# A block's second SiLU, gating and split behind the next block's first product, in a fused encoder layer on one core

## The chip, the core and the metric

The kernel is one launch on one core of a Trainium2 chip. A core has TensorE (PE in the rows, with its weight loads apart as PEld), VectorE (DVE), ScalarE (ACT), GpSimd (POOL) and SyncE (SP, which here issues the DMAs). Each engine works through its own instructions in the order in which the program wrote them, and waits on semaphores for the others. The metric is the device time of the launch in microseconds: 1426.03 us, the median of three runs (1423.1 to 1428.0).

## The reference, cut to what matters

One encoder layer over 1024 positions of 1024 features, fp32: two kinds of attention, then a gated MLP with a depthwise convolution over three positions. The change is in the MLP:

```python
h = modulate(rms_norm(x), shift_ffn, scale_ffn)
gate, val = jnp.split(causal_depthwise_conv(h @ w_up, conv_w, conv_b), 2, axis=-1)
x = x + gate_ffn[:, None, :] * ((jax.nn.silu(gate) * val) @ w_down)
...
return rms_norm(x) * final_g
```

`w_up` is 1024 x 5632 and `w_down` 2816 x 1024, so there are 22 blocks of 128 gate columns, each with its 128 value columns.

## The kernel before

The MLP fills the second half of the launch. Positions lie along the free axis in two halves of 512 (`lo`, `hi`). Every fp32 operand of a matmul is split into a rounded high part and the remainder (`wh` and `wl`, `ah` and `al`, `dh` and `dl`), and a product is made of three matmuls per 128 rows of depth: high by high, high by low, low by high. A split takes a rounding copy and a subtraction.

The blocks from the third on (`act_fast`, `fb` = 2 to 21, 20 of them) use seven products of 12 matmuls instead of eight, by sums and differences of weights and of activations that are made beforehand. They go into four PSUM tiles, X, Y, W and Z (all named `up` in the trace):

- first product, X = w0 by B11; ACT copies X to SBUF (L1154, `y<-up`);
- second, Y; DVE adds it to that copy (L1164), which is the first half of the gate columns; ACT starts its convolution (L1133), DVE ends it (two rows of L1137), ACT takes the SiLU (L1172);
- a second product *into X* (w4 by T2, `up<-Tc,wh` in the rows), which adds onto what stands there: it can't begin before ACT has read X (L1154). ACT copies X again (L1170);
- the "third product" of the change, again into X (w5 by B12, line 1181, `up<-h,wh`): it needs L1170 done. ACT copies X a third time (L1182);
- W, Z and Z again: DVE takes them off (L1188, L1198, L1209), ACT and DVE do the convolutions of the value columns and of the second half of the gate columns, ACT takes the second half's SiLU (L1214).

`gated` (line 1067) multiplies one half of gate and value (L1070, DVE), rounds the product to `ah` (L1071, a cast on DVE before) and subtracts for `al` (L1072, DVE). It is called for the first half at line 1207 and for the second at line 1218.

The way down of block b (`down`, 16 tiles of three matmuls, `dnf<-...` in the rows, and a DVE addition L1262 into `x2`) is spread between the products of block b + 1 by `tiles(n)`; `NDOWN` says how many tiles go into each place, four more stand at the block's end. Tiles 0 to 3 and 8 to 11 use the first half's `ah`, `al`, the others the second half's; tiles 0 to 7 use the first half of the `w_down` columns (`dh`, `dl`), 8 to 15 the second. These are made from a loaded piece `modt` by POOL (L1237, times the gate), ACT (L1239, `dh`) and POOL (L1240, `dl`). Three `modt` buffers exist and two hold constants, so the load of the second half starts when L1240 of the first is done. The splits of the next block's `w_up` (ACT L1092, POOL L1094) and the sums of its weights (POOL L1101 to L1106) run in between; the split behind the first product makes w5 and w6.

All of these calls are kept in the order written (`ko`, `keep_in_program_order`), engine by engine, so the order of the Python statements is the order on each engine.

Of the kernel before, what the change touches and what calls it, by code (L numbers as in the profile page):

```python
# [13 lines left out]
AF = mybir.ActivationFunctionType  # L14
# [12 lines left out]
NP = 8  # L27
FF = 2816
NF = FF // P
NDOWN = 2, 3, 2, 2, 3  # L30
NLAST = 2, 2, 0, 0, 0
NTWO = 0, 4, 2, 3, 3
TL = sum(NLAST)
# [22 lines left out]
def build(nc, tc, t, ctx):  # L56
    sy, ve, sc, gp, te = nc.sync, nc.vector, nc.scalar, nc.gpsimd, nc.tensor
    cnt = [0]

    def mk(pool, shape, dt, tag):  # L60
        cnt[0] += 1
        return pool.tile(shape, dt, name=f"{tag}_{cnt[0]}", tag=tag, bufs=BUFS.get(tag, 1))
# [61 lines left out]
    def load_w(src, shape):  # L124
        raw = mk(wst, shape, F32, "raw")
        r = sy.dma_start(raw, src)
        if hold[0]:
            tc.keep_in_program_order(r)
        return raw
# [98 lines left out]
    ko = tc.keep_in_program_order  # L228
# [834 lines left out]
    def act_tiles(last):  # L1063
        return [[mk(p2, [P, HALF], F32R, "h2") if last else mk(p3, [P, HALF], F32R, n) for _ in range(2)]
                for n in ("ah", "al")]

    def gated(yg, yv, hf, ah, al):

        cc = slice(hf * HALF, (hf + 1) * HALF)
        ko(ve.tensor_mul(yg[:, cc], yg[:, cc], yv[:, cc]))  # L1070
        ko(ve.tensor_copy(ah[hf], yg[:, cc]))  # L1071
        ko(ve.tensor_sub(al[hf], yg[:, cc], f(ah[hf])))  # L1072


# [10 lines left out]
    def weight_sums(fb, w):  # L1085

        rv, rg = (load_w(t["w_up"][b], [P, KB, P]) for b in (NF + fb, fb))
        g0, g1, v0, v1 = rg[:, 0:4], rg[:, 4:8], rv[:, 0:4], rv[:, 4:8]

        def split(tag, pl, raw, cuts=None):  # L1090
            wh, wl = (mk(pl, list(raw.shape), F32R, tag + x) for x in "hl")
            ko(sc.copy(wh, raw))  # L1092
            for a, z in cuts or [(0, raw.shape[1])]:
                late.append(lambda a=a, z=z: ko(gp.tensor_sub(wl[:, a:z], raw[:, a:z], f(wh[:, a:z]))))  # L1094
            late.pop(-len(cuts) if cuts else -1)()
            w.extend([x[:, n:n + 4] for x in (wh, wl)] for n in range(0, raw.shape[1], 4))

        yield
        split("w", p0, rg)
        yield  # L1100
        ko(gp.tensor_sub(g0, g0, v0))  # L1101
        ko(gp.tensor_add(v0, v0, v1))
        yield
        split("wq", p3, v1)
        ko(gp.tensor_sub(v1, v1, g0))
        ko(gp.tensor_sub(g1, v1, g1))  # L1106
        yield
        split("w", p0, rv, fb == 2 and ((4, 8), (0, 4)))
        yield
        split("w", p0, rg, fb == 2 and ((0, 4), (4, 8)))  # L1110

    late = []

    def roundrobin(*its):
        while True:
# [4 lines left out]
    def run(it, n):  # L1120
        for _ in range(n):
            next(it, None)

    def product(ps, w, b, start):
        n = 0
        for kb in LO:
            for x, y in ((0, 0), (0, 1), (1, 0)):
                ko(te.matmul(ps, w[x][:, kb], b[kb][y], start=start and n == 0, stop=n == 11, skip_group_check=True))  # L1128
                n += 1

    def conv_steps(y, src, b, a, z):
        b = slice(b, b + 1)
        ko(sc.activation(y[:, a:z], src[:, a:z], AF.Identity, scale=cw[2][:, b], bias=cb[:, b]))  # L1133
        for d in (1, 2):
            yield
            o = max(a, d)
            ko(ve.scalar_tensor_tensor(y[:, o:z], src[:, o - d:z - d], cw[2 - d][:, b], y[:, o:z], ALU.mult, ALU.add))  # L1137

    def act_fast(fb, w, dn, nw, nw1, ld, ld1, act, after, last):


        X, Y, W, Z = (mk(fps[0][1], [P, HALF], F32, "up") for _ in range(4))
        lo, hi = slice(0, HALF), slice(HALF, S)
        n = NLAST if last else NTWO if fb == 2 else NDOWN
        cg, cv = (mk(p2, [P, S], F32, "y") for _ in range(2))
        nx = lambda it: next(it, None)

        def tiles(n, c=iter(()), dn=dn):
            for _ in range(n):
                nx(dn)  # L1150
                nx(c)

        product(X, w[0], B11, True)
        ko(sc.copy(cg[:, lo], X))  # L1154
        if fb == 2:
            second_act()
        yg, yv = (mk(p2, [P, S], F32, "y") for _ in range(2))
        nx(nw)
        nx(nw1)
        product(Y, w[1], B21, True)  # L1160
        while late:
            late.pop(0)()
        nx(ld)
        ko(ve.tensor_add(cg[:, lo], Y, cg[:, lo]))  # L1164
        c = conv_steps(yg, cg, fb, 0, HALF)
        if fb > 2:
            nx(c)
        tiles(n[0], c)
        product(X, w[4], T2, False)
        ko(sc.copy(cg[:, hi], X))  # L1170
        run(c, 9)
        ko(sc.activation(yg[:, lo], yg[:, lo], AF.Silu))  # L1172
        nx(nw1)
        nx(ld)
        if fb == 2:
            nx(ld)
        if last:
            nx(ld1)
            fg.append(load_w(bass.AP(t["final_g"].tensor, 0, [[0, P], [1, D]]), [P, D]))
        tiles(n[1])  # L1180
        product(X, w[5], B12, False)
        ko(sc.copy(cv[:, hi], X))  # L1182
        nx(nw1)
        if last:
            nx(ld1)
        tiles(n[2])
        product(W, w[2], T4, True)
        ko(ve.tensor_sub(cv[:, lo], cv[:, hi], W))  # L1188
        c = conv_steps(yv, cv, NF + fb, 0, HALF)
        nx(c)  # L1190
        if last:
            nx(ld1)
        nx(nw1)
        tiles(n[3], c)
        run(c, 1 if last else 9)
        nx(ld1)
        product(Z, w[3], T1, True)
        ko(ve.tensor_sub(cv[:, hi], cv[:, hi], Z))  # L1198
        run(c, 9)
        c = conv_steps(yv, cv, NF + fb, HALF, S)  # L1200
        nx(c)
        nx(ld1)
        nx(nw1)
        tiles(n[4], c)
        run(c, 9)
        act += act_tiles(last)
        gated(yg, yv, 0, *act)
        product(Z, w[6], B22, False)
        ko(ve.tensor_sub(cg[:, hi], cg[:, hi], Z))  # L1209
        c = conv_steps(yg, cg, fb, HALF, S)  # L1210
        nx(c)
        nx(ld1)
        tiles(2 if last else 4, c, after)
        ko(sc.activation(yg[:, hi], yg[:, hi], AF.Silu))  # L1214
        nx(ld1)
        if last:
            tiles(3, dn=after)
        gated(yg, yv, 1, *act)

    gbc = []  # L1220

# [43 lines left out]
    def down(a, w, order):  # L1265
        for tb, hf in order:
            down_mm(tb, hf, [a], [w])
            yield
# [37 lines left out]
    def conv_half(y, src, b, hf):  # L1306
        b = slice(b, b + 1)
        a, z = hf * HALF, (hf + 1) * HALF
        ko(sc.activation(y[:, a:z], src, AF.Identity, scale=cw[2][:, b], bias=cb[:, b]))
        for d in (1, 2):  # L1310
            yield
            ko(ve.scalar_tensor_tensor(y[:, a + d:z], src[:, 0:HALF - d], cw[2 - d][:, b], y[:, a + d:z], ALU.mult,
                                       ALU.add))

    def conv_join(y, before, b):

        b = slice(b, b + 1)
        for d in (1, 2):
            o = y[:, HALF:HALF + d]
            ko(ve.scalar_tensor_tensor(o, before[:, HALF - d:HALF], cw[2 - d][:, b], o, ALU.mult, ALU.add))  # L1320
# [14 lines left out]
    lo, hi = slice(0, HALF), slice(HALF, S)  # L1335
# [42 lines left out]
    yg, yv = (mk(p2, [P, S], F32, "y") for _ in range(2))  # L1378
    act = act_tiles(False)
# [6 lines left out]
    for kb in LO:  # L1386
        split2(T1[kb], sums[kb])
    gated(yg, yv, 0, *act)
    run(ld, 1)

# [46 lines left out]
    yg, yv = (mk(p2, [P, S], F32, "y") for _ in range(2))  # L1437
# [6 lines left out]
    dn = down(act, wd, by_half)  # L1444
# [16 lines left out]
    def second_act(yg=yg, yv=yv, act=act1):  # L1461
        conv_join(yg, g0, 1)
        ko(sc.activation(yg, yg, AF.Silu))
        run(conv_half(yv, v0, NF + 1, 0), 9)
        conv_join(yv, v0, NF + 1)
        for hf in range(2):
            gated(yg, yv, hf, *act)

    act, wd = act1, wd1
    for fb in range(2, NF):  # L1470
        last = fb == NF - 1
        w1 = []
        nw1 = iter(()) if last else weight_sums(fb + 1, w1)
        wd1 = [], []
        ld1 = load_down(fb, wd1, last)
        dn, act1 = down(act, wd, by_half), []
        if last:
            dn = islice(dn, TL)
            out = chain(dn, down_last((act, act1), (wd, wd1)))
        act_fast(fb, w, dn, nw, nw1, ld, ld1, act1, out if last else dn, last)  # L1480
        act, w, nw, wd, ld = act1, w1, nw1, wd1, ld1
# [39 lines left out]
```

## Time and profile before

| what | number |
|---|---|
| median of three runs | 1426.03 us |
| the profiled execution, its own time | 1425.51 us |
| its span, first to last instruction | 1423.5 us |
| PE busy over the span | 1309.2 us (92%), 6644 matmuls |
| DVE busy | 1176.2 us (83%) |
| ACT busy | 617.2 us (43%) |
| POOL busy | 864.9 us (61%) |

The table is the page's head and first part. A share of busy time is a mean over stages with different limits, and a matmul's end is modelled, so a PE that is shown busy may still lose time: the starts of two matmuls, one behind the other, tell what was lost between them. Rows of the timeline give the start in us from the span's start, how long it took, engine, line, operation, what it writes and reads, and at the end, in brackets, the idle time before it and who ended it; x2 at the end of a row merges two instructions.

### The profile page before, as it was taken

How to read it: one execution, taken by the hardware profiler on the slowest of the kernel's cores; microseconds unless marked ns; L12 is line 12 of the kernel's file. 1: busy time of each engine (PE TensorE's matmuls, PEld its weight loads, DVE VectorE, ACT ScalarE, POOL GpSimd, SP SyncE). 2: the span in 40 equal slices, each digit the busy share in tenths (PEclk: the TensorE clock that was granted, in tenths of full speed). 3: DMA queues.
4: the chain of work that ended last, by engine and by line, in shares of the span. 5: the costliest groups of instructions: out<-in, count | busy, mean ns of one | idle time of the engine just before them, and what ended most of it. 6: DMA issues, size and time to landing. Idle time of an engine off the chain costs nothing.

```text
span 1423.5 us, 19845 instructions
## 1 busy us (share of the span) xinstructions
PE 1309.2 (92%) x6644; PEld 1083.0 (76%) x6644; DVE 1176.2 (83%) x1967; ACT 617.2 (43%) x1270; POOL 864.9 (61%) x760
## 2 busy tenths in 40 slices
PE   4889999999899978798887999999999999999996
PEld 2688998898778966676665877777777778777774
DVE  7858777677778868876889889999998889899887
ACT  5647567575545433333432333323333333333334
POOL 4646576765333436563578667776676677667664
PEclk9999999999999999899998999999999999999998
DMA  8534433414665686665011111111111111211213
GB/s 311 180 100 112 104 88 85 119 49 120 166 167 144 179 263 197 217 193 193 22 45 36 47 52 45 45 45 60 52 54 58 45 45 45 60 52 49 62 37 119
DMA packets 80047, 144.57 MB, mean 102 GB/s; under 512 B 10041, under 2 KB 36809, under 8 KB 79946
## 3 DMA queue, kind: packets, MB, share of 16 engines
q1 hardware_dynamic: 79946, 143.31, 33.9%
q8 instruction: 53, 0.87, 0.3%
q14 instruction: 48, 0.39, 0.1%
HBM read 102.89 MB, written 18.88 MB: 86 GB/s over the span
## 4 chain that ended last, share of the span: by engine, by line
PE 43%; DVE 35%; ACT 7%; issue 5%; DMA 5%; POOL 4%; SPq 1%; POOLq 0%; DVEq 0%; ACTq 0%
PE mm L136 14%; PE up L1128 12%; DVE y L1137 8%; PE T L136 6%; PE dnf L136 6%; DVE x L1262 4%; PE S L136 3%; ACT y L1133 3%; DVE ah L1071 3%; DVE y L1070 2%; DVE adaw L254 1%; DVE macc L918 1%; PE up L1302 1%; POOL wl L121 1%; DVE al L1072 1%
## 5 line engine op out<-in xcount | busy, mean ns | idle before, releaser
L1262 DVE TENSOR_TENSOR x<-dnf,x 128x512 f32<-128x512 f32 x340 | 222.5, 679 | 1.6 <-PE dnf L136 1.6
L1137 DVE SCALAR_TENSOR_TENSOR y<-y,sm,y 128x512 f32<-128x512 f32 (+2 forms) x160 | 187.3, 1171 | 28.8 <-ACT y L1133 28.7
L1128 PE MATMUL up<-h,wh 128*128 128x512 f32 x640 | 199.7, 393 | 2.6 <-ACT y L1170 1.8
L1094 POOL TENSOR_TENSOR wl<-raw,wh 128x1024 fp32r<-128x1024 f32 (+1 forms) x62 | 160.1, 2583 | 66.1 <-ACT wh L1092 59.5
L1133 ACT ACTIVATE y<-y,sm 128x512 f32<-128x512 f32 x80 | 65.3, 817 | 254.7 <-DVE y L1209 133.4
L136 PE MATMUL mm<-H,wh 128*128 128x512 f32 x448 | 150.2, 403 | 0.0
L1128 PEld LDWEIGHTS up<-h,wh 128*128 128x128 f32 x640 | 119.7, 189 | 31.1 <-ACT y L1170 5.2
L136 PE MATMUL dnf<-dh,ah 128*128 128x512 f32 x336 | 133.5, 397 | 10.0 <-DVE x L1262 8.8
L136 PE MATMUL dnf<-dl,ah 128*128 128x512 f32 x336 | 134.0, 399 | 3.7 <-POOL dl L1240 2.5
L802 POOL TENSOR_TENSOR pb<-pb,kt 128x512 f32<-128x512 f32 (+2 forms) x96 | 89.4, 945 | 77.0 <-DVE kt L799 50.0
L136 PE MATMUL dnf<-dh,al 128*128 128x512 f32 x336 | 132.6, 395 | 0.9 <-DVE al L1072 0.9
L1128 PE MATMUL up<-h,wl 128*128 128x512 f32 x320 | 125.3, 392 | 0.0
L822 DVE TENSOR_TENSOR ptl<-T,pth 128x512 fp32r<-128x512 f32 (+2 forms) x192 | 98.5, 517 | 30.7 <-ACT pth L821 29.0
L821 ACT CAST pth<-T 128x512 fp32r<-128x512 f32 (+2 forms) x192 | 87.4, 457 | 62.3 <-PE T L136 60.9
L795 POOL TENSOR_SCALAR pb<-pb,ri 128x640 f32<-128x640 f32 (+2 forms) x64 | 45.4, 711 | 106.2 <-DVE ri L794 67.7
L136 PE MATMUL mm<-wh,H 128*128 128x256 f32 x512 | 102.8, 292 | 6.6 <-DVE vs L511 6.6
L799 DVE TENSOR_TENSOR_SCAN kt<-kt 128x128 f32<-128x128 f32 (+3 forms) x64 | 98.2, 1534 | 9.8 <-ACT kt L784 9.4
L1128 PE MATMUL up<-Tc,wh 128*128 128x512 f32 x320 | 100.9, 396 | 4.6 <-ACT y L1154 4.5
L1240 POOL TENSOR_TENSOR dl<-modt,dh 128x512 fp32r<-128x512 f32 x42 | 65.3, 1554 | 64.3 <-ACT dh L1239 64.3
L1237 POOL TENSOR_TENSOR modt<-modt,modt 128x512 f32<-128x512 f32 x44 | 68.8, 1563 | 58.2 <-DMA modt<-w_down 58.2
L136 PE MATMUL S<-kh,qs 128*128 128x384 f32 (+5 forms) x352 | 99.5, 364 | 4.6 <-ACT pb L778 4.4
L136 PE MATMUL T<-ident,pb 128*128 128x128 f32 x528 | 91.1, 277 | 8.8 <-POOL pb L802 3.5
(214 smaller groups left out, 3451.1 us busy)
## 6 DMA issues: line engine op xcount, KB each, us to landing
raw<-w_up SPq DMA_DIRECT2D x44, 512.0 KB, 3.6
rawm<-ada SPq DMA_DIRECT2D x128, 128.0 KB, 2.4
qs<-ex SPq DMA_DIRECT2D x104, 128.0 KB, 2.5
modt<-w_down SPq DMA_DIRECT2D x44, 256.0 KB, 2.7
adaw<-ada SPq DMA_DIRECT2D x16, 512.0 KB, 5.7
raw<-w_qk SPq DMA_DIRECT2D x16, 512.0 KB, 3.6
kh<-ex SPq DMA_DIRECT2D x56, 128.0 KB, 2.6
tbd<-wh SPq DMA_DIRECT2D x18, 256.0 KB, 2.6
```

What stands on the lines that cost most here:

```text
L136: r = fn(*a, **k)
L799: ve.tensor_tensor_scan(r, r, r, 1.0, ALU.mult, ALU.bypass)
L802: gp.tensor_mul(pt[:, a:b], pt[:, a:b], kt[:, a + 1:b + 1])
L821: sc.copy(dh, tp[:, 0:b - a])
L822: ve.tensor_sub(dl, tp[:, 0:b - a], f(dh))
L1094: late.append(lambda a=a, z=z: ko(gp.tensor_sub(wl[:, a:z], raw[:, a:z], f(wh[:, a:z]))))
L1128: ko(te.matmul(ps, w[x][:, kb], b[kb][y], start=start and n == 0, stop=n == 11, skip_group_check=True))
L1133: ko(sc.activation(y[:, a:z], src[:, a:z], AF.Identity, scale=cw[2][:, b], bias=cb[:, b]))
L1137: ko(ve.scalar_tensor_tensor(y[:, o:z], src[:, o - d:z - d], cw[2 - d][:, b], y[:, o:z], ALU.mult, ALU.add))
L1237: ko(gp.tensor_mul(raw, raw, gbc[hf]))
L1240: ko(gp.tensor_sub(wl, raw, f(wh)))
L1262: r = ve.tensor_add(xc, ps, xc)
```

## The change

Three edits. The second half's SiLU, gating and split of a block are wrapped in `second_half` and put on a list; the next block calls them right behind its first product's copy, before its second product is written. (`second_act`, which did the same by a special case for the second block, comes through the same list.) The last block calls them where they were. One tile of the way down is moved from the place ahead of the third product to the place behind it (`NDOWN`). And the rounding copy to `ah` in `gated` goes from DVE to ACT, in all 44 uses.

```diff
--- before.py
+++ after.py
@@ -27,7 +27,7 @@
 NP = 8
 FF = 2816
 NF = FF // P
-NDOWN = 2, 3, 2, 2, 3
+NDOWN = 2, 2, 3, 2, 3
 NLAST = 2, 2, 0, 0, 0
 NTWO = 0, 4, 2, 3, 3
 TL = sum(NLAST)
@@ -1068,7 +1068,7 @@
 
         cc = slice(hf * HALF, (hf + 1) * HALF)
         ko(ve.tensor_mul(yg[:, cc], yg[:, cc], yv[:, cc]))
-        ko(ve.tensor_copy(ah[hf], yg[:, cc]))
+        ko(sc.copy(ah[hf], yg[:, cc]))
         ko(ve.tensor_sub(al[hf], yg[:, cc], f(ah[hf])))
 
 
@@ -1109,7 +1109,7 @@
         yield
         split("w", p0, rg, fb == 2 and ((0, 4), (4, 8)))
 
-    late = []
+    late, rest = [], []
 
     def roundrobin(*its):
         while True:
@@ -1152,8 +1152,7 @@
 
         product(X, w[0], B11, True)
         ko(sc.copy(cg[:, lo], X))
-        if fb == 2:
-            second_act()
+        rest.pop()()
         yg, yv = (mk(p2, [P, S], F32, "y") for _ in range(2))
         nx(nw)
         nx(nw1)
@@ -1211,11 +1210,17 @@
         nx(c)
         nx(ld1)
         tiles(2 if last else 4, c, after)
-        ko(sc.activation(yg[:, hi], yg[:, hi], AF.Silu))
-        nx(ld1)
+
+        def second_half(between=lambda: None):
+            ko(sc.activation(yg[:, hi], yg[:, hi], AF.Silu))
+            between()
+            gated(yg, yv, 1, *act)
+
         if last:
-            tiles(3, dn=after)
-        gated(yg, yv, 1, *act)
+            second_half(lambda: (nx(ld1), tiles(3, dn=after)))
+        else:
+            nx(ld1)
+            rest.append(second_half)
 
     gbc = []
 
@@ -1467,6 +1472,7 @@
             gated(yg, yv, hf, *act)
 
     act, wd = act1, wd1
+    rest.append(second_act)
     for fb in range(2, NF):
         last = fb == NF - 1
         w1 = []
```

The order on ACT at a block's boundary, before: L1214 is the second half's SiLU, L1154 the copy of the next block's first product, L1092 a weight split, L1239 a `dh`, L1133 and L1170 the convolution's start and the second copy of X.

```order
L1133 ACTIVATE y_10917<-y_10902,sm_74 128x512
L1239 CAST dh_11047<-modt_11045 128x512
L1214 ACTIVATE y_10917<-y_10917 128x512
L1154 COPY y_11143<-up_11139 128x512
L1092 CAST wh_11160<-raw_10925 128x1024
L1239 CAST dh_11110<-modt_11108 128x512
L1133 ACTIVATE y_11158<-y_11143,sm_74 128x512
L1170 COPY y_11143<-up_11139 128x512
```

The same place now (L1244, L1215 and L1169 are the lines that were L1239, L1214 and L1170):

```order
L1071 CAST ah_11085<-y_10917 128x512
L1133 ACTIVATE y_10917<-y_10898,sm_74 128x512
L1244 CAST dh_11047<-modt_11045 128x512
L1154 COPY y_11139<-up_11135 128x512
L1215 ACTIVATE y_10917<-y_10917 128x512
L1071 CAST ah_11086<-y_10917 128x512
L1092 CAST wh_11160<-raw_10925 128x1024
L1244 CAST dh_11110<-modt_11108 128x512
L1133 ACTIVATE y_11158<-y_11139,sm_74 128x512
L1169 COPY y_11139<-up_11135 128x512
```

The copy and the SiLU have changed places, and two casts have come in: one ahead of the gate's last convolution, one ahead of the weight split.

On PE, ahead of the third product, before (each tile is three rows; `ah_9881` is the second half's):

```order
L136 MATMUL dnf_10014<-dl_9843,ah_9880 128x512
L136 MATMUL dnf_10014<-dh_9842,al_9882 128x512
L136 MATMUL dnf_10019<-dh_9842,ah_9881 128x512
L136 MATMUL dnf_10019<-dl_9843,ah_9881 128x512
L136 MATMUL dnf_10019<-dh_9842,al_9883 128x512
L1128 MATMUL up_9934<-h_1942_8203,wh_9955 128x512
L1128 MATMUL up_9934<-h_1943_8204,wh_9955 128x512
```

The same place now:

```order
L136 MATMUL dnf_10014<-dl_9843,ah_9880 128x512
L136 MATMUL dnf_10014<-dh_9842,al_9882 128x512
L1128 MATMUL up_9930<-h_1942_8203,wh_9955 128x512
L1128 MATMUL up_9930<-h_1943_8204,wh_9955 128x512
...
L1128 MATMUL up_9930<-h_1946_8207,wl_9956 128x512
```

The first tile that uses the second half's `ah` stands behind the 12 matmuls of the third product now; between the second and the third product into X there are two tiles instead of three. DVE's order is the one before without its casts, POOL's and SP's are unchanged.

## Rows read from the trace of the kernel before

**Rows 1.** Windows, 18 loop blocks: length; busy PE, PEld, DVE, ACT, POOL; clock; DMA.
```profile
803.16:1364.10 560.94, 551.63 (x2378) 440.79 (x2377) 503.24 (x614) 190.91 (x270) 386.77 (x217) 1.00 0.17 51
```

**Rows 2.** Timeline of PE (start, us, line, op): one block, 1021.52 to 1034.10.
```profile
1021.52 0.61 PE L1128 MATMUL up<-h,wh 128*128 128x512 f32 x2
...
1026.96 0.39 PE L136 MATMUL dnf<-dh,ah 128*128 128x512 f32 x1
...
1027.44 0.50 PE L136 MATMUL dnf<-dl,ah 128*128 128x512 f32 x1
...
1028.49 0.40 PE L136 MATMUL dnf<-dh,al 128*128 128x512 f32 x1
...
1029.13 0.73 PE L1128 MATMUL up<-Tc,wh 128*128 128x512 f32 x2 [0.24 <-ACT y L1154]
...
1034.10 0.64 PE L1128 MATMUL up<-h,wh 128*128 128x512 f32 x2
```

**Rows 3.** Timeline of ACT in the same block.
```profile
1024.63 0.81 ACT L1133 ACTIVATE y<-y,sm 128x512 f32<-128x512 f32 x1 [6.76 <-DVE y L1209]
...
1025.35 0.60 ACT L1239 CAST dh<-modt 128x512 fp32r<-128x512 f32 x1
...
1027.97 0.63 ACT L1214 ACTIVATE y<-y 128x512 f32<-128x512 f32 x1 [2.02 <-DVE y L1137]
...
1028.51 0.57 ACT L1154 COPY y<-up 128x512 f32<-128x512 f32 x1
...
1033.40 0.56 ACT L1170 COPY y<-up 128x512 f32<-128x512 f32 x1
```

**Rows 4.** Timeline of DVE in the same block.
```profile
1019.56 1.18 DVE L1070 TENSOR_TENSOR y<-y,y 128x512 f32<-128x512 f32 x1
...
1020.77 2.50 DVE L1071 CAST ah<-y 128x512 fp32r<-128x512 f32 x1
...
1023.30 0.69 DVE L1072 TENSOR_TENSOR al<-y,ah 128x512 fp32r<-128x512 f32 x1
...
1023.91 0.68 DVE L1209 TENSOR_TENSOR y<-y,up 128x512 f32<-128x512 f32 x1
...
1030.23 1.81 DVE L1072 TENSOR_TENSOR al<-y,ah 128x512 fp32r<-128x512 f32 x1
...
1031.96 0.68 DVE L1164 TENSOR_TENSOR y<-up,y 128x512 f32<-128x512 f32 x1
```

**Rows 5.** Timeline of POOL in the same block.
```profile
1020.14 2.84 POOL L1094 TENSOR_TENSOR wl<-raw,wh 128x1024 fp32r<-128x1024 f32 x1
...
1026.03 1.36 POOL L1240 TENSOR_TENSOR dl<-modt,dh 128x512 fp32r<-128x512 f32 x1 [3.05 <-ACT dh L1239]
...
1030.20 1.29 POOL L1237 TENSOR_TENSOR modt<-modt,modt 128x512 f32<-128x512 f32 x1 [2.81 <-DMA modt<-w_down]
```

**Rows 6.** Timeline of PE in the last block, ahead of its third product.
```profile
1375.60 0.39 PE L136 MATMUL dnf<-dh,al 128*128 128x512 f32 x1
...
1376.39 0.73 PE L1128 MATMUL up<-h,wh 128*128 128x512 f32 x2 [0.40 <-ACT y L1170]
```

**Rows 7.** Timeline of DVE ahead of the block that starts at 1052.51.
```profile
1051.47 2.28 DVE L1070 TENSOR_TENSOR y<-y,y 128x512 f32<-128x512 f32 x1
...
1053.79 0.43 DVE L1071 CAST ah<-y 128x512 fp32r<-128x512 f32 x1
```

**Rows 8.** Timeline of ACT in the block that starts at 1052.51.
```profile
1064.37 0.57 ACT L1170 COPY y<-up 128x512 f32<-128x512 f32 x1
```

**Rows 9.** Groups by line on DVE in the loop (count, busy us, mean ns).
```profile
L1071 DVE CAST ah<-y 128x512 fp32r<-128x512 f32 x37 | 44.9, 1212 | 1.3
```

**Rows 10.** Waits in 706 to 804 us (us in total, times, longest).
```profile
PE up L1302 <- DVE wl L1326: 2.4, 1, 2.4
...
PE dnf L136 <- DVE ah L1071: 1.2, 1, 1.2
```

**Rows 11.** Timeline of ACT in the loop's opening block.
```profile
773.91 1.05 ACT L1092 CAST wh<-raw 128x1024 fp32r<-128x1024 f32 x1
```

## Prediction

> **What bounds the kernel now.** I read the waits of PE first, then the busy times of the loop, then the timelines of one block, engine by engine. The loop of 18 whole blocks takes 560.94 us, 31.16 us a block, and holds 2378 matmuls, 132 a block [rows 1]. PE is shown busy for 551.63 of that [rows 1], but ends are modelled; starts tell more. The 24 matmuls from 1021.52 to 1026.96 took 5.44 us, 0.2267 us each [rows 2], so 132 would take 29.92 us. A block loses 31.16 - 29.92 = 1.24 us on PE, 22 us in the loop, and that is all that this change can win there. The granted clock is 1.00 throughout the loop [rows 1], so none of it is clock.
>
> Where it goes is in the gaps between starts, in every block at the same places [rows 2]. From 1026.96 to 1027.44 are 0.48 us, 0.25 too many: the second matmul of a tile waits for `dl`, which POOL ends at 1026.03 + 1.36 = 1027.39 [rows 5]. The matmul behind such a stop comes 0.11 late too. From 1028.49 to 1029.13 are 0.64, 0.41 too many, and again 0.11 behind it: the second product into X waits for the first copy of X. That copy (L1154) starts at 1028.51 although X was complete at about 1024.4 (the twelfth matmul starts 11 x 0.2267 behind 1021.52 and takes 0.39); it stood behind the SiLU L1214, which waited for DVE until 1027.97 [rows 3]. So 0.36 for `dl` and 0.52 for the copy; the rest of the 1.24 is a few hundredths at other places and some blocks with a longer wait for `dl` or a late load.
>
> **The change part by part.** *SiLU behind the copy.* L1154 now stands behind the `dh` cast alone, which ends at 1025.35 + 0.60 = 1025.95 [rows 3]. The copy ends by 1026.6, two microseconds before PE wants X. The 0.52 us goes. The SiLU keeps its time, since it waits for DVE and not for the copy.
>
> *The cast on ACT.* On DVE it takes 1.21 us in the mean, 37 times in this stretch [rows 9], 0.43 where nothing is in its way [rows 7] and 2.50 where a POOL operation runs [rows 4]: it began at 1020.77, POOL's L1094 ran until 1022.98 [rows 5], and it ended 0.29 after that. On ACT nothing shows this cast; the nearest row is another rounding copy of 128x512 at 0.60 [rows 3]. With 0.04 for each handover (L1209 ends at 1024.59, L1133 starts at 1024.63 [rows 3, 4]), the first half's `al` (L1072) may begin at 1020.74 + 0.04 + 0.60 + 0.04 = 1021.42 instead of 1023.30. But L1072 has the same trouble as the cast: at 1030.23 it began 0.03 behind POOL's L1237, which ended at 1031.49, and took until 1032.04, 0.55 after that [rows 4, 5]. Behind L1094 it will end at 1022.98 + 0.55 = 1023.53. Before it ended at 1023.99 [rows 4]. The cast's 2.50 us buys 0.46, no more: the wait for POOL goes from one instruction to the next. L1209, the convolution's start L1133, `dh` and `dl` follow 0.46 earlier; `dl` at 1026.93, ahead of the 1027.19 at which PE wants it. The 0.36 goes as well.
>
> In the second half the cast saves nothing: `al` begins while POOL runs L1237 either way. L1237 follows the first half's `dl` by a load, 1027.39 to 1030.20 [rows 5], so it too comes 0.46 earlier, and with it `al`, L1164, L1133 and the second copy of X, L1170: from 1033.40 + 0.56 = 1033.96 [rows 3] to 1033.50.
>
> *The moved tile.* Before, the third product started at 1034.10 [rows 2], 0.14 behind that copy: it was all but waiting. Now it is wanted 0.36 + 0.52 earlier for the two stops, 0.14 for the rest, and 0.68 (three matmuls) earlier for the tile that no longer stands ahead of it: at 1026.96 + 24 x 0.2267 = 1032.40 (two tiles, 12 matmuls, two tiles). The copy ends at 1033.50 and PE starts 0.05 behind it, as at 1029.13. PE waits from 1032.40 to 1033.55, 1.15 us, and 0.11 behind. Behind PE everything waits: W is the next product that DVE needs. The last block of the kernel before shows it already: there no tile was in that place beyond two, and between 1375.60 and 1376.39 lie 0.79 us, 0.56 too many, although the two stops ahead of it were still there [rows 6]. So a block comes to 29.92 + 1.15 + 0.11 = 31.18 us, against 31.16: the two stops have become one.
>
> *POOL's lead.* This sum holds while the first half's multiplication (L1070) is issued before POOL starts L1094: 1019.56 against 1020.14 [rows 4, 5], 0.58 us of lead. POOL's run of weight work now starts 0.46 earlier in the block than before, against DVE's work, which is tied to W and so to PE. Little of the lead is left. Where it is lost, L1070 itself waits for L1094: 2.28 us instead of 1.18, as at 1051.47 [rows 7], one of five such rows in the loop. Then POOL is idle behind it, the cast costs 0.43 before and 0.60 now, so everything behind is some 0.18 later than in that block instead of 0.46 earlier. There the second copy started at 1064.37 and ended at 1064.94 [rows 8]; with 0.18 more, and the 0.05, the third product starts at 1065.17, 12.66 us behind its block's start. Unhindered it would be 48 x 0.2267 = 10.88. Such a block takes 29.92 + 12.66 - 10.88 + 0.11 = 31.81 us, 0.65 more than the mean before.
>
> I take half of the blocks each way: 31.50 us, (31.50 - 31.16) x 18 = +6.1 us.
>
> *The tail.* The last block's two casts lie on PE's way to the end; ACT's 0.60 and a handover of 0.04 for DVE's 0.43, twice: +0.4 us.
>
> *The opening (706 to 804 us).* PE waited 2.4 us there for a split behind such a cast, and 1.2 for a cast itself [rows 10]. ACT's casts can give back up to these 3.6. Against that, in the loop's opening block the weight copy that ran at 773.91 [rows 11] now stands behind both gatings, which end near 780, some 6 us later, and its POOL subtraction, the loads that reuse its buffer and the next `dl` behind it: that may eat all of the gain and, by what was gained, no more than a microsecond beyond it. Between -3.6 and +1, I take -1.0.
>
> Sum: 6.1 + 0.4 - 1.0 = +5.5 us on the profiled execution's 1425.51: **1431.0 us**. That execution stands 0.5 us under the median of three, which I leave out.
>
> **The rivals.** *The forecast*, the lead lost in some blocks and kept in others: 1427 to 1436.
>
> *No change*: POOL never gets ahead, each block takes 31.18: 18 x 0.02 + 0.4 - 1.0, 1425.3 us. For it speaks that 13 of 18 blocks before kept the lead; against it that the lead is now about 0.1.
>
> *Faster*: the first half's `al`, ready at 1021.42, doesn't meet L1094 but slips ahead of it, in a block where POOL is 1.3 us later than shown. Then it ends near 1022.1, 1.9 earlier than before, the second copy at about 1032.1, ahead of the 1032.40 at which it is wanted, and the block loses nothing: -1.24. If half of the blocks do so, 1425.5 - 11.2 - 0.6 = 1413.7. For it speaks that DVE loses 44.9 us of casts [rows 9] of the 503 us that it is busy [rows 1]; against it that L1094 ran from 1020.14 to 1022.98 [rows 5], with 1021.42 in the middle of it, and that POOL's lead grows.
>
> *Slower in every block*: the lead is lost throughout, 18 x 0.65 + 0.4 - 1.0 = +11.1, 1436.6 us. It decides when POOL starts L1094 before 1019.56 in the block's time.
>
> The Trainium skill (Perfetto Trace Analysis, Optimizing Scalar/DVE Operations) says that an operation for which DVE has a performance mode is faster there, and that handing work to ScalarE may make sense if DVE is saturated. By its first half the cast loses time in each use, and the kernel goes the way of the last rival, to 1436.6; by its second half DVE, busy 90% of the loop [rows 1], gains. The trace has both: 0.43 alone, 2.50 beside POOL [rows 4, 7].
>
> **How the numbers follow.** The forecast has 0.45, no change 0.25, faster 0.17, slower in every block 0.13. A measurement of this kernel tells 0.3% from no change, 4.3 us. Faster by more: 0.15 of the third and 0.05 of the opening's gain on top of the second, 0.20. Slower by more: 0.35 of the forecast and all 0.13 of the last, 0.48. Between them 0.32. The range leaves out most of the third case and the upper edge of the last: 1420 to 1438.
>
> **What would show it.** Right: L1154's successor directly behind `dh`, and no gap ahead of `up<-Tc,wh`; a gap of 1.2 to 1.8 us ahead of the third product in nearly every block, ended by ACT's second copy; L1070 of the first half at 2.28 more often than five times; the loop's block at 31.2 to 31.8. Wrong: a third product that starts within 0.2 of its wish, or `al` of the first half ending before POOL's L1094; then the block is near 30 and the kernel faster. If the gap ahead of the third product is there but ended by POOL (the low part of w5), the place is right and the chain is not.

## The result and the profile after

The changed kernel takes 1432.77 us (median of 12 runs) against 1424.84 us for the kernel before (12 runs): ratio 1.0051, 95% interval 1.0037 to 1.0065, 7.3 us slower. One run of the changed kernel, at 2571 us far from all others, is in its median and not in the ratio; the other eleven have a median of 1432.64. The forecast was 1431.0. The profiled execution took 1430.78 us, 5.3 more than that of before. The loop of 18 blocks takes 6.1 us more, and opening and tail take less, as the windows show (columns as in [rows 1]):

```profile
802.92:1369.93 567.01, 547.73 (x2378) 444.76 (x2377) 477.49 (x576) 212.34 (x306) 382.28 (x216) 1.00 0.17 51
```

567.01 / 18 = 31.50 us a block against 31.16; the median block went from 31.00 to 31.40. DVE is busy 26 us less, ACT 21 more [rows 1]: the load was moved as meant, and the loop is longer. The page's groups (busy us, mean ns; idle before them and what ended most of it) say where. The second product into X no longer waits; the third product, L1128 on `h`, does:

```profile
L1128 PE MATMUL up<-h,wh 128*128 128x512 f32 x640 | 202.3, 398 | 20.9 <-ACT y L1169 20.0
...
L1128 PE MATMUL up<-Tc,wh 128*128 128x512 f32 x320 | 99.8, 393 | 0.0
```

(Behind L1154 most line numbers are one lower: L1169 is the second copy of X, L1170 before; L1208 was L1209; `modt`, `dh`, `dl` and the additions are L1242, L1244, L1245 and L1267.) The block that starts at 1022.15, on PE, answers to [rows 2]:

```profile
1027.59 0.39 PE L136 MATMUL dnf<-dh,ah 128*128 128x512 f32 x1
...
1028.97 0.63 PE L1128 MATMUL up<-Tc,wh 128*128 128x512 f32 x2
...
1032.85 0.39 PE L136 MATMUL dnf<-dh,al 128*128 128x512 f32 x1
1034.31 0.73 PE L1128 MATMUL up<-h,wh 128*128 128x512 f32 x2 [1.07 <-ACT y L1169]
```

From 1027.59 to 1028.97 are 1.38 us for six matmuls (6 x 0.2267 = 1.36): both old stops, at `dl` and at the copy of X, are gone. From 1032.85 to 1034.31 are 1.46, 1.23 too many. Worked out from starts like that in every block, the new stop is 0.57 to 1.36 us in 17 blocks and 2.45 in one. ACT in that block [rows 3], then DVE [rows 4], then POOL [rows 5]:

```profile
1026.12 0.58 ACT L1154 COPY y<-up 128x512 f32<-128x512 f32 x1
...
1032.97 0.82 ACT L1133 ACTIVATE y<-y,sm 128x512 f32<-128x512 f32 x1 [0.59 <-DVE y L1163]
1033.69 0.56 ACT L1169 COPY y<-up 128x512 f32<-128x512 f32 x1
```

```profile
1020.54 2.28 DVE L1070 TENSOR_TENSOR y<-y,y 128x512 f32<-128x512 f32 x1
1023.57 0.69 DVE L1072 TENSOR_TENSOR al<-y,ah 128x512 fp32r<-128x512 f32 x1 [0.74 <-ACT ah L1071]
...
1042.19 0.69 DVE L1187 TENSOR_TENSOR y<-y,up 128x512 f32<-128x512 f32 x1 [2.10 <-PE up L1128]
```

```profile
1019.42 2.85 POOL L1094 TENSOR_TENSOR wl<-raw,wh 128x1024 fp32r<-128x1024 f32 x1
...
1039.22 2.40 POOL L1094 TENSOR_TENSOR wl<-raw,wh 128x1024 fp32r<-128x1024 f32 x1 [2.98 <-ACT wh L1092]
```

The copy that PE waits for was free to read X at about 1031.9 (the product's last matmul starts at 1031.49 and takes 0.39); it stands on ACT behind the convolution's start L1133, which waits for DVE. And POOL's L1094 starts ahead of the gating's L1070, which is shown at 2.28 us because it waits L1094 out: so in 16 of the 18 blocks, 5 of 18 before.

### The profile page after: what moved, and what is told of

Its sections match the earlier page's. It is cut to its first block, busy times and chain, and to the rows that moved or that the text cites. A ratio compares the mean times of both kernels' runs of the same rounds, so it can differ in the third digit from the quotient of the medians.

```text
span 1429.0 us, 19866 instructions
## 1 busy us (share of the span) xinstructions
PE 1303.8 (91%) x6644; PEld 1084.5 (76%) x6644; DVE 1142.0 (80%) x1923; ACT 643.8 (45%) x1314; POOL 858.7 (60%) x760
## 4 chain that ended last, share of the span: by engine, by line
DVE 39%; PE 35%; ACT 9%; POOL 6%; issue 5%; DMA 4%; SPq 1%; POOLq 0%; ACTq 0%; DVEq 0%
PE mm L136 14%; DVE y L1137 9%; PE up L1128 8%; PE T L136 7%; DVE x L1267 5%; ACT y L1133 4%; DVE y L1070 4%; PE S L136 3%; DVE al L1072 3%; PE dnf L136 3%; DMA rawm<-ada 2%; ACT ah L1071 2%; DVE adaw L254 1%; DVE macc L918 1%; POOL wl L121 1%
## 5 line engine op out<-in xcount | busy, mean ns | idle before, releaser
L1267 DVE TENSOR_TENSOR x<-dnf,x 128x512 f32<-128x512 f32 x340 | 226.8, 681 | 3.1 <-PE dnf L136 1.7
L1128 PE MATMUL up<-h,wh 128*128 128x512 f32 x640 | 202.3, 398 | 20.9 <-ACT y L1169 20.0
L1137 DVE SCALAR_TENSOR_TENSOR y<-y,sm,y 128x512 f32<-128x512 f32 (+2 forms) x160 | 189.7, 1186 | 26.7 <-ACT y L1133 26.6
L1094 POOL TENSOR_TENSOR wl<-raw,wh 128x1024 fp32r<-128x1024 f32 (+1 forms) x62 | 159.9, 2580 | 68.9 <-ACT wh L1092 52.5
L1128 PEld LDWEIGHTS up<-h,wh 128*128 128x128 f32 x640 | 120.0, 190 | 54.1 <-ACT y L1169 28.6
L1133 ACT ACTIVATE y<-y,sm 128x512 f32<-128x512 f32 x80 | 65.3, 816 | 163.8 <-DVE y L1197 61.9
L1128 PE MATMUL up<-h,wl 128*128 128x512 f32 x320 | 125.8, 393 | 0.1
L1245 POOL TENSOR_TENSOR dl<-modt,dh 128x512 fp32r<-128x512 f32 x42 | 65.5, 1561 | 75.0 <-ACT dh L1244 75.0
L1242 POOL TENSOR_TENSOR modt<-modt,modt 128x512 f32<-128x512 f32 x44 | 66.8, 1518 | 56.9 <-DMA modt<-w_down 56.9
L1128 PE MATMUL up<-Tc,wh 128*128 128x512 f32 x320 | 99.8, 393 | 0.0
```

What stands on the lines that cost most here:

```text
L1242: ko(gp.tensor_mul(raw, raw, gbc[hf]))
L1245: ko(gp.tensor_sub(wl, raw, f(wh)))
L1267: r = ve.tensor_add(xc, ps, xc)
```

## The experiments

The three edits first, apart and in pairs; "S" is the deferred SiLU, "C" the cast on ACT, "T" the moved tile. Ratios are against the kernel before, run beside each.

| edits | time, us | ratio | 95% interval | L1070 at 2.28 |
|---|---|---|---|---|
| none | 1424.3 to 1426.2 | 1 | | 5 of 18 |
| S | 1426.22 | 1.0015 | 1.0001 to 1.0029 | 7 |
| C | 1456.71 | 1.0229 | 1.0212 to 1.0247 | 17 |
| T | 1429.42 | 1.0036 | 1.0024 to 1.0048 | 15 |
| S, C | 1419.44 | 0.9965 | 0.9953 to 0.9978 | 6 |
| S, T | 1429.94 | 1.0037 | 1.0022 to 1.0051 | 15 |
| S, C, T (the change) | 1432.77 | 1.0051 | 1.0037 to 1.0065 | 16 |

**S and C, the tile put back.**

```diff
-NDOWN = 2, 2, 3, 2, 3
+NDOWN = 2, 3, 2, 2, 3
```

> The changed kernel with NDOWN as it was (2, 3, 2, 2, 3): SiLU deferred and cast on ACT stay, the tile of the way down goes back ahead of the third product. Theory (the moved tile costs): in the changed kernel PE stops 0.57 to 1.36 us plus 0.11 ahead of the third product in all 18 blocks, because that product now starts one tile (1.81 us) sooner than the second copy of X is ready. With the tile back, most of it goes and nothing takes its place but a few tenths at the dl stop: 0.8 to 1.0 us less in a block than the 31.50 of the changed kernel, 30.5 to 30.7, or 15 to 18 us in all: 1415 us (1411 to 1420), faster than before by 0.4 to 0.9%. Rival (the lost lead of POOL costs): POOL still starts its subtraction of the third weight (L1094) ahead of the gating's, L1070 still takes 2.28 us, and what the tile hid comes out at the dl stop of PE: 31.3 to 31.5 per block, 1428 to 1433 us.

1419.44 us, 0.9965: the theory's time holds, near the upper end of its range: the kernel is 13 us faster than the changed one and 0.35% faster than before. Its price does not: the mean block is 30.88 us, 0.62 less than in the changed kernel and not 0.8 to 1.0, for two smaller stops remain (waits of PE over the loop: us in total, times, longest):

```profile
PE dnf L136 <- DVE x L1267: 6.0, 17, 0.5
PE dnf L136 <- POOL dl L1245: 2.2, 7, 0.4
```

The first is the third tile ahead of the third product, which needs a PSUM buffer that DVE's addition has yet to read.

**T alone.** The kernel before with `NDOWN = 2, 2, 3, 2, 3`.

> The kernel before with NDOWN alone changed (2, 2, 3, 2, 3). Theory (the moved tile costs by itself): a stop of about 1.0 us ahead of the third product in each of the 18 blocks, as in the changed kernel; the stop at the copy of X (0.52) and the dl stop (0.36) shrink by part of it, since DVE and ACT gain what PE loses: 0.2 to 0.5 us more in a block, 1429 to 1434 us, slower by 0.3 to 0.6%. Rival (the third-product stop comes from the SiLU's new place, which holds up ACT ahead of the second copy): no stop there, 1424 to 1426 us.

1429.42 us, 1.0036: the theory's time. The stop ahead of the third product comes without any change to the SiLU or the cast, so these are not its cause, and the copy's stop stays beside it:

```profile
PE up L1128 <- ACT y L1170: 10.5, 18, 2.0
PE up L1128 <- ACT y L1154: 3.6, 15, 0.3
```

Starts give 0.51 to 0.67 us for it in 16 blocks (1.73 and 2.18 in the other two), half of the changed kernel's and of the theory's: here the copy's stop ahead of it, 0.24 to 0.44 us by starts, still delays PE's wish. The `dl` stop is gone or under 0.1 us in all but three blocks.

**C alone.** The kernel before with the cast on ACT:

```diff
-        ko(ve.tensor_copy(ah[hf], yg[:, cc]))
+        ko(sc.copy(ah[hf], yg[:, cc]))
```

> The kernel before with the gating's cast (L1071) on ACT alone; SiLU and tile as before. Theory (the cast on ACT is the part that gains): the dl stop of PE (0.36 with its share of starting up) goes, the copy stop of 0.52 stays or shrinks: 0.3 to 0.5 us less in a block, 1416 to 1420 us, faster by 0.3 to 0.6%. Rival (the cast on ACT loses POOL's lead, so L1070 waits out POOL's L1094 for 2.28 us, and the dependent subtraction L1072 is no earlier): the dl stop stays at 0.3 or grows, 1425 to 1430 us.

1456.71 us, 2.29% slower: both expectations fail. ACT and PE in one block:

```profile
1038.54 0.63 ACT L1214 ACTIVATE y<-y 128x512 f32<-128x512 f32 x1 [2.02 <-DVE y L1137]
1040.39 0.62 ACT L1071 CAST ah<-y 128x512 fp32r<-128x512 f32 x1 [1.22 <-DVE y L1070]
1040.92 0.58 ACT L1154 COPY y<-up 128x512 f32<-128x512 f32 x1
```

```profile
1041.55 0.73 PE L1128 MATMUL up<-Tc,wh 128*128 128x512 f32 x2 [1.79 <-ACT y L1154]
```

The cast comes between SiLU and copy on ACT. It waits for DVE's L1070, and the copy behind it with it. PE stops 1.94 to 2.09 us there in every block, plus 0.11, in place of 0.52. In 10 of the 18 blocks PE then runs slow for a while. Of the block whose stop ends at 1073.56 the windows show the granted clock at full speed (2.4 GHz) at first and at half (1.2) soon after, third number from the right:

```profile
1073.56:1074.80 1.24, 1.24 (x5) 1.05 (x6) 1.24 (x2) 1.24 (x2) 0.87 (x2) 1.00 0.05 13
1076.40:1077.50 1.10, 1.10 (x4) 0.89 (x3) 1.10 (x2) 0.00 (x0) 1.10 (x2) 0.50 0.00 0
```

Such a block takes 33.6 us, the others 32.0, so some 16 of the 32 us come with the lower clock (an estimate, 10 times 1.6). So the deferred SiLU is what makes the cast on ACT bearable: with both edits the copy of X stands ahead of SiLU and cast. The effects don't add: S +2 us, C +32, both together -5.

**S alone.** The changed kernel with the old `NDOWN` and the cast back on DVE.

> The changed kernel with NDOWN as it was and the cast back on DVE, so that the SiLU with its gating behind the copy of X is alone. Theory (the copy stop of PE was slack of the DVE chain, not work): the 0.52 us at the copy of X goes, but DVE sets the pace at the gating, whose chain is no shorter, so the dl stop or the third-product stop grows by the same: 30.9 to 31.2 per block, 1423 to 1428 us. Rival (the copy stop was the bound by itself): 0.52 times 18 = 9.4 us less, 1415 to 1417 us, faster by 0.6%.

1426.22 us, 1.0015: the theory holds. The copy's stop is gone, and PE loses the same elsewhere:

```profile
PE up L1128 <- ACT y L1169: 4.4, 6, 1.5
PE dnf L136 <- DVE x L1267: 3.2, 11, 0.3
PE dnf L136 <- POOL dl L1245: 2.9, 6, 0.9
```

**S and T.** The changed kernel with the cast back on DVE.

> The changed kernel with the cast of the gating (L1071) back on DVE; SiLU deferred and tile moved stay. It closes the square: with the tile back the cast was worth 1426.22 - 1419.44 = 6.8 us. Theory (each part acts by its own wait, so the cast is worth the same here): 1432.8 + 6.8, about 1437 to 1441 us. Rival (where the third product's stop sets the pace, an earlier gating buys nothing, or costs POOL's lead): the time stays within 2 us of the changed kernel, 1431 to 1435 us.

1429.94 us, and its interval overlaps that of the changed kernel: the theory falls, and the time is 1 us below the rival's range too. With the tile back the cast was worth 6.8 us, here nothing that can be told from zero. DVE shows why:

```profile
1020.94 2.28 DVE L1070 TENSOR_TENSOR y<-y,y 128x512 f32<-128x512 f32 x1
1023.26 0.43 DVE L1071 CAST ah<-y 128x512 fp32r<-128x512 f32 x1
1023.72 0.69 DVE L1072 TENSOR_TENSOR al<-y,ah 128x512 fp32r<-128x512 f32 x1
```

Where L1070 has waited POOL out, the cast costs DVE 0.43, not 2.50; from the end of L1070 to the start of L1072 are 0.50 us here, and 0.75 with the cast on ACT (1020.54 + 2.28 to 1023.57).

**The copy ahead of the convolution's start.** The changed kernel with L1133 issued behind the second copy (the convolution's two steps on DVE move behind the tiles with it, so DVE's order changes too):

```diff
-        if fb > 2:
-            nx(c)
-        tiles(n[0], c)
+        tiles(n[0])
```

> The changed kernel with the start of the convolution (the activation L1133 that waits for DVE's L1163) issued on ACT behind the second copy of X and not ahead of it, so that the copy waits for the product alone. Theory (the copy is only the last of two waits there: POOL's subtraction for the third product's weights ends at 1034.52 in the block where the product is wanted at 1032.40 and the copy is done at 1034.25): the wait passes from ACT to POOL, PE still stops about 1 us, 0 to 0.3 us less in a block, 1427 to 1433 us. Rival (ACT's queue is the whole stop): 1.0 to 1.1 us less in each of 18 blocks, 1413 to 1416 us.

1429.49 us, 1.0037 (1.0024 to 1.0049): the theory holds. PE, and its waits over the loop:

```profile
1031.76 0.63 PE L1128 MATMUL up<-h,wh 128*128 128x512 f32 x2
1033.20 0.50 PE L1128 MATMUL up<-h,wl 128*128 128x512 f32 x1 [0.81 <-POOL wl L1094]
```

```profile
PE up L1128 <- POOL wl L1094: 13.2, 17, 0.9
PE up L1128 <- ACT y L1167: 2.1, 3, 1.1
```

The product now starts when it wants to and stops at its third matmul for the low part of its weights, which POOL ended at 1030.38 + 2.77 = 1033.15:

```profile
1030.38 2.77 POOL L1094 TENSOR_TENSOR wl<-raw,wh 128x1024 fp32r<-128x1024 f32 x1
```

So one tile earlier the third product has two things late, not one, and taking one of them away bought 3 us by the medians, less than the two intervals can tell.

**POOL's subtraction in two.** The changed kernel with the split's L1094 ahead of the first half's gating made of two instructions of 512 columns:

```diff
-            for a, z in cuts or [(0, raw.shape[1])]:
+            for a, z in two[:-1] if two and not cuts else []:
+                ko(gp.tensor_sub(wl[:, a:z], raw[:, a:z], f(wh[:, a:z])))
+            for a, z in cuts or [two[-1] if two else (0, raw.shape[1])]:
...
-        split("w", p0, rv, fb == 2 and ((4, 8), (0, 4)))
+        split("w", p0, rv, fb == 2 and ((4, 8), (0, 4)), ((0, 4), (4, 8)))
```

> The changed kernel with POOL's subtraction L1094 that starts ahead of the first half's gating (2.85 us, 1024 columns) cut in two of 512 columns, so that DVE can start between them. Theory (L1070 waits the whole POOL instruction out, 2.28 in 16 of 18 blocks, and what is behind it on DVE, ACT and POOL up to the third product is late by that): L1070 takes 1.2 to 1.7 and everything behind it is 0.5 to 1.0 earlier; the third product's stop shrinks by as much: 0.4 to 0.9 us less in a block, 1417 to 1426 us. Rival (POOL is itself the last at the third product, and one more instruction on it costs 0.3): same or slower, 1431 to 1438 us.

1415.04 us, 0.9929 (0.9913 to 0.9946): 17.7 us less than the changed kernel, the theory holds and is too small. DVE and POOL ahead of the block that starts at 1047.8:

```profile
1046.55 1.18 DVE L1070 TENSOR_TENSOR y<-y,y 128x512 f32<-128x512 f32 x1
```

```profile
1045.44 1.74 POOL L1094 TENSOR_TENSOR wl<-raw,wh 128x512 fp32r<-128x512 f32 x1
1047.13 1.74 POOL L1096 TENSOR_TENSOR wl<-raw,wh 128x512 fp32r<-128x512 f32 x1
```

POOL still starts ahead of L1070 in 15 of the 18 blocks, but L1070 ends 0.55 behind the first half (1047.18) and not behind the whole: 1.18 us in all 18 blocks. Everything up to the second copy moves with it: by starts, the stop ahead of the third product goes from 1.2 to 0.6 us in the median block, and the block's mean is 30.65 us.

**Both repairs**: the tile back and the subtraction in two.

> The changed kernel with the tile back (NDOWN 2, 3, 2, 2, 3) and POOL's subtraction L1094 ahead of the gating cut in two: both repairs together. With the tile back alone (1419.44) PE still stops 0.38 to 0.67 us ahead of the third tile of the second group and up to 0.55 at the dl stop. Theory (both stops hang on the gating, late by DVE's wait for the whole POOL subtraction: L1072 2.07, L1070 1.18 or 2.28): 0.2 to 0.6 us less in a block, 1409 to 1416 us. Rival (DVE's and POOL's own work sets these stops, not the wait for each other): 1418 to 1423 us.

1406.96 us, 0.9875 (0.9857 to 0.9894), better than expected and 1.25% faster than the kernel before. Windows of the loop, and PE's waits in it:

```profile
800.02:1342.16 542.14, 541.09 (x2378) 444.42 (x2376) 454.61 (x576) 213.43 (x305) 398.25 (x236) 1.00 0.17 53
```

```profile
PE up L1130 <- ACT y L1171: 0.6, 2, 0.3
PE dnf L136 <- DVE x L1269: 0.4, 2, 0.2
```

30.12 us a block, where 132 matmuls take 29.92: the loop is bound by PE now.

**The subtraction in two, in the kernel before.**

> The kernel before with POOL's subtraction L1094 ahead of the first half's gating cut in two of 512 columns, nothing else; SiLU, cast and tile as before. It asks whether the wait of DVE for the whole POOL instruction cost the kernel before as well. Theory (it did: there the cast L1071 waits the 2.85 us out, 2.50 in place of 0.43, and al, the dl stop and the copy behind the SiLU are late by it): the cast or L1070 takes about 1 us less, the dl stop of 0.36 goes and the copy stop of 0.52 shrinks: 0.4 to 0.7 us less in a block, 1412 to 1418 us. Rival (the copy stop is set by ACT's order alone and the gain shows only where the SiLU is deferred): 1419 to 1424 us.

1421.09 us, 0.9970 (0.9954 to 0.9986): the rival's time. The cast on DVE took 1.40 in place of 2.50,

```profile
1047.38 1.40 DVE L1071 CAST ah<-y 128x512 fp32r<-128x512 f32 x1
1048.81 1.66 DVE L1072 TENSOR_TENSOR al<-y,ah 128x512 fp32r<-128x512 f32 x1
```

but L1072 then waits for the second half (1.66), and the copy of X still stands behind the SiLU: by starts the `dl` stop of the median block halves, from 0.26 to 0.13, and the copy's stays, 0.42 against 0.43. The cut is worth 0.3% here and 1.2% in the changed kernel.

**Both subtractions in two**, with the tile back.

> The changed kernel with the tile back, and both of POOL's 1024-column subtractions in a block cut in two: also the one beside the second half's gating, where L1072 takes 1.5 to 1.7 in place of 0.69 in the blocks in which it meets POOL. With the first cut alone the time was 1406.96 us, and PE stopped 0.1 to 0.5 us in 9 of 18 blocks, at the third tile or the third product of the second group. Theory (what is left there is again DVE waiting for POOL): the blocks come to 29.95 to 30.05 on average in place of 30.13, 1402 to 1406 us. Rival (what is left is POOL's own work, 0.3 us longer by the cut, and ACT's order): 1406 to 1411 us.

1405.46 us, 0.9860 (0.9837 to 0.9882). It can't be told from the run with one cut (the intervals overlap, and the profiled blocks take 30.13 us in the mean against 30.12). With 0.2 us a block left over PE's own work there was little to find.

## Why the prediction was right, and where it was not

*The two old stops go*: right, at the places named, in nearly every block (the `dl` stop is 0.54 us in one block and under 0.17 in the others).

*The moved tile puts a stop ahead of the third product, ended by ACT's second copy*: right. In the two blocks that kept POOL's lead the stop was 1.06 us, against 1.15 worked out, and these blocks took 31.14 and 31.18 us, against 31.18. That it is the tile's doing is shown by the runs with the tile alone (+5 us) and with it back (-13 us). Named among the signs but not priced: POOL's low part is as late as the copy, by the run with the copy first.

*The lead is lost in half of the blocks, at 31.81 us each*: wrong in both factors, and the two errors cancelled by luck. It was lost in 16 of 18. Of these, 15 blocks took 31.36 us in the mean, 0.20 over the mean before and not 0.65. The step that failed is the price, taken from the block that starts at 1052.51, where L1070 began 1.04 us ahead of the block's first product [rows 7]. In the changed kernel it begins 1.61 ahead (1020.54 against 1022.15), 0.57 earlier in the block, and the third product starts 12.16 us behind the block's start, not 12.66. Losing the lead holds L1070 up by less than in the block that gave the price: from W's row L1187 (L1188 before) to L1070 are 9.33 us in most blocks that kept it, 10.25 to 10.42 in those that lost it before, and 9.46 to 9.94 in 14 of the 16 that lost it here. "31.50 a block" came out for a sum of other terms: two blocks at the old mean, fifteen at +0.20, and one at 34.25.

That last one, 3.1 of the loop's 6.1 us, is a late load, for which the forecast has no term. POOL and ACT there:

```profile
1126.72 1.28 POOL L1242 TENSOR_TENSOR modt<-modt,modt 128x512 f32<-128x512 f32 x1 [4.68 <-DMA modt<-w_down]
```

```profile
1128.04 0.62 ACT L1244 CAST dh<-modt 128x512 fp32r<-128x512 f32 x1 [2.05 <-POOL modt L1242]
1128.56 0.81 ACT L1133 ACTIVATE y<-y,sm 128x512 f32<-128x512 f32 x1
1129.28 0.56 ACT L1169 COPY y<-up 128x512 f32<-128x512 f32 x1
```

The copy stands on ACT behind `dh` too, which waits for the load. The block at the same place before took 32.15 us with a stop of 1.08 by starts. How much of the median's +7.3 us such blocks make can't be read from one profile; the median block's +0.40 by 18 gives 7.2 without them.

*Why so many blocks lose the lead.* I took POOL's work to come 0.46 us earlier against DVE's; that isn't it. POOL's L1094 in the middle of the block is released by an ACT cast that waits for the load of `w_up`, and starts 4.98 us behind the third product in the median block, with the tile moved as with the tile back (5.03 before). It comes earlier in the block, 17.14 us behind the start against 17.66, only as the third product does. But the tile that left the place ahead of the third product now stands between that product and W, on which DVE's gating hangs. From the third product's start to DVE's L1187 are 7.88 us in the block shown (1034.31 to 1042.19), and 7.88 to 7.92 in all 18 but the one with the late load; with the tile back they are 7.08 to 7.15. In one block of that run:

```profile
1066.94 0.69 DVE L1187 TENSOR_TENSOR y<-y,up 128x512 f32<-128x512 f32 x1 [1.73 <-PE up L1128]
```

```profile
1065.43 2.40 POOL L1094 TENSOR_TENSOR wl<-raw,wh 128x1024 fp32r<-128x1024 f32 x1 [3.75 <-ACT wh L1092]
```

There DVE's L1187 starts 1.51 us behind that L1094, and at the block's end the lead is kept; in the changed kernel's block it starts 2.97 behind (1042.19 against 1039.22), and the lead is lost. This distance parts all 144 loop blocks of the eight kernels that leave POOL's subtraction whole: the lead is kept up to 2.23 us and lost from 2.24 on. With the tile back 11 of 18 blocks lie within 0.13 us of that edge, and the 0.77 us by which DVE comes later with the tile moved push nearly all of them over it. The table agrees over whole kernels: 15 or 16 blocks with the tile moved, 5 to 7 without, whatever SiLU and cast do; the cast alone is apart (17), with a stop of PE in every block.

*The cast buys 0.46 us in the first half*: about so, where the lead is kept. With S and the tile in its old place it was worth 6.8 us, 0.38 a block; with the lead lost it is worth nothing that shows, as DVE's rows of that run show. *No rival* was right; the last one had the blocks (16 of 18) and not the price.

*Opening and tail*: -1.0 and +0.4 were forecast, -0.24 (802.92 against 803.16) and -0.4 measured (59.07 us behind the last whole block against 59.48). In the opening the waits that the casts were charged with gave back 1.9 us of the 3.6 [rows 10], and other waits took more. PE's waits there in the changed kernel:

```profile
PE dnf L136 <- DVE x L1267: 11.1, 5, 3.4
PE dnf L136 <- POOL dl L1245: 2.0, 1, 2.0
PE up L1307 <- DVE wl L1331: 1.5, 1, 1.5
```

The split's wait fell from 2.4 to 1.5 and the cast's from 1.2 to 0.2; the waits for DVE's additions rose from 8.8 to 11.1, and the one for `dl` is new. Why these rose no run here shows.

The Trainium skill (SBUF — State Buffer, Who interferes with whom) says that a DVE instruction with two inputs in SBUF and a GpSimd instruction that reads SBUF exclude each other, for the whole of the one that began first. The runs agree where POOL began first: with the same lost lead, cutting POOL's instruction in two took L1070 from 2.28 to 1.18 us and 17.7 us off the kernel.

## What to carry to other kernels

Before you move work on one engine's queue, list what stands behind it there and what that waits for: the same cast costs 32 us in one place and gains 7 in another. Where two engines exclude each other, look at the length of the blocking instruction on the other engine before you shorten the blocked one: in the changed kernel, cutting POOL's in two gave 17.7 us, more than any edit on DVE or ACT did. It gave 5 in the kernel before, where another stop stayed. And a right sum isn't a right model: count how many blocks are in each state and what each costs.

## What was not expected of the hardware

The lead takes one of two values. In 18 blocks of the changed kernel POOL's L1094 starts 1.11 or 1.12 us ahead of L1070 (16 times) or 0.59 behind it (twice); so it is in the other kernels, with one exception. The two differ by 1.70, one POOL instruction. DVE's L1137 ahead of the gating, which reads two buffers, waits for POOL too, and goes on when the one that runs is done. DVE and POOL in the changed kernel:

```profile
1048.09 1.59 DVE L1137 SCALAR_TENSOR_TENSOR y<-y,sm,y 128x512 f32<-128x512 f32 x1 [0.28 <-ACT y L1133]
...
1051.90 2.29 DVE L1070 TENSOR_TENSOR y<-y,y 128x512 f32<-128x512 f32 x1
```

```profile
1047.83 1.30 POOL L1106 TENSOR_TENSOR raw<-raw,raw 128x512 f32<-128x512 f32 x1
1049.08 1.75 POOL L1242 TENSOR_TENSOR modt<-modt,modt 128x512 f32<-128x512 f32 x1
1050.78 2.86 POOL L1094 TENSOR_TENSOR wl<-raw,wh 128x1024 fp32r<-128x1024 f32 x1
```

L1137 began 0.26 behind L1106 and ended 0.55 behind its end (1049.13 + 0.55 = 1049.68). With the tile back it ran into L1105, one instruction sooner (POOL 1072.67 to 1073.96, DVE's L1137 ending at 1074.51), and kept the lead. L1070 isn't free in a block that keeps the lead either: it takes 1.18 us where the second half's takes 0.67, and ends 0.54 behind the POOL instruction ahead of L1094 (1075.62 + 1.74 = 1077.36). DVE and POOL in that block with the tile back:

```profile
1076.73 1.17 DVE L1070 TENSOR_TENSOR y<-y,y 128x512 f32<-128x512 f32 x1
```

```profile
1075.62 1.74 POOL L1242 TENSOR_TENSOR modt<-modt,modt 128x512 f32<-128x512 f32 x1
```

So a shift of a few tenths becomes one of 1.70 or none: a chain of waits between DVE and POOL has steps, and a sum of small shifts can't price it.
